# Joining two of three products of the query, key and value projections into one 512-column matmul

## The chip, the cores and the metric

The kernel runs on one core of one Trainium2 chip. The metric is the device time of one execution in microseconds; the time before is a median of three runs. The profile is of one more execution, whose own time stands beside it.

## The reference, cut to what matters

The whole program is one inference step of two trunk layers: a retention and pooling layer and an attention layer, each followed by a feed-forward network (FFN). It works on 9 tiles of 128 tokens: tile 0 holds the context tokens, tiles 1 to 8 the latent tokens. The change lies in the projection of the attention layer, all in float32:

```
def attn_project(h, w_qkv, q_gain, k_gain):
    B, T, _ = h.shape
    q, k, v = jnp.split(h @ w_qkv, [N_HEADS * HEAD_DIM, (N_HEADS + KV_HEADS) * HEAD_DIM], axis=-1)
    q = rmsnorm(q.reshape(B, T, N_HEADS, HEAD_DIM), q_gain)
    k = rmsnorm(k.reshape(B, T, KV_HEADS, HEAD_DIM), k_gain)
    v = v.reshape(B, T, KV_HEADS, HEAD_DIM)
    return q, k, v
```

`h` has 1,152 rows of 1,024 elements, `w_qkv` 1,536 columns: 1,024 for eight query heads, 256 for two key heads and 256 for two value heads. Queries and keys of the latent tokens are then rotated by their place in a grid (`axial_rope`), and the attention follows.

## The kernel before, in words

**Products in parts.** A float32 product is made from parts in the matmul type `fp32r`: each operand is split into a high part (a cast, on ScalarE) and a low part (the rest, a subtraction on VectorE; `split`, lines 155 to 157). `mm3` (line 174) then adds three products into one PSUM region: high by high, high by low, low by high. Its matmuls stand on line 179, which all other stages but the FFN input use too.

**The projection.** The columns of `w_qkv` are taken in six blocks of 256 (`blocks`): value, query heads 0 and 1, key, and three more query blocks. One call of `qkv_step(bi, t)` makes the 256 columns of block `bi` for token tile `t`. The inner dimension of 1,024 is taken in 8 slices of 128, so a step has 8 x 3 = 24 matmuls, each with 128x128 of `h` as the loaded weights and 256 columns of `w_qkv` moving. There are 6 x 9 = 54 steps. The high part of a weight block lies in 2,048 elements of each partition of `RR`, and the low part in the next 2,048; there are two such pairs of regions, and `load_blk` fills one from DRAM through `RAW`, with a cast and a subtraction per half.

**Behind the matmuls.** A step's result stands in one of PSUM's banks of 512 float32 columns (banks 0 to 3 in turn; for the last block 3 and 7) and uses 256 of them. In a value step ScalarE and VectorE split it into `VH` and `VL`; tile 0 is copied to `vctx` and stored. In a query or key step ScalarE squares and sums each head (line 1175), POOL works out the reciprocal root (`rstd_of`, lines 184 and 185), VectorE scales by it and by the gain into `qn` (line 1182), and for latent tokens VectorE and POOL rotate (lines 1190 to 1194) with two temporary halves `ra` and `rb`. Its `tail` (transposes on TensorE, line 1198, and a copy, line 1207) waits in the list `pend` and is issued behind the matmuls of the second step after it. `qn` has three buffers (`qnb`) and `ra`/`rb` two (`rab`), taken in turn.

**Order.** Steps run in two phases. In the first, the value block and the first query block run for three token tiles at a time, while the transposed input `h` is still being made: `go` issues h steps, with transposes on TensorE (line 258), ScalarE's scale and shift into a temporary (line 261) and VectorE's split (lines 263 and 264). In the second phase the other four blocks run over all nine tiles, with the cached keys (line 1223), the cached values and the context's attention between them. In the last block the first score products (`scores`, line 179 again, 512 and 256 columns), with maximum, exponential (line 1291) and so on, run between steps. Within each engine the framework that builds the program arranges the instructions and places all waits; an engine then runs its own queue in order.

Of the kernel before, what the change touches and what calls it, by code (L numbers as in the profile page):

```python
# [17 lines left out]
KD = 8  # L18
# [46 lines left out]
def hybrid_step_kernel(ctx: ExitStack, tc: tile.TileContext, a: dict, outs: list):  # L65
    nc = tc.nc
# [7 lines left out]
    RR = base.tile([128, 26624], F32R, name="RR")  # L74
# [36 lines left out]
    def bank(i, n=1):  # L111
        return PS[:, i * 512:(i + n) * 512]

    def h_hi(g):
        return RR[:, g * 6144:g * 6144 + 3072].rearrange("p (k t) -> p k t", k=KD)

    def h_lo(g):
        return RR[:, g * 6144 + 3072:g * 6144 + 6144].rearrange("p (k t) -> p k t", k=KD)
# [14 lines left out]
    def w_pair(i):  # L133
        b = RR[:, 18432 + i * 2048:18432 + (i + 2) * 2048]
        return (b[:, 0:2048].rearrange("p (k f) -> p k f", k=KD),
                b[:, 2048:4096].rearrange("p (k f) -> p k f", k=KD))

    def tok(t):
        return O[:, :, t * 128:(t + 1) * 128]

# [2 lines left out]
    def sm(n=1):  # L143
        i = ring["sm"]
        if i + n > 64:
            i = 0
        ring["sm"] = i + n
        return SM[:, i:i + n]
# [6 lines left out]
    def split(hi, lo, src):  # L155
        nc.scalar.copy(hi, src)  # L156
        nc.vector.tensor_sub(lo, src, hi)  # L157
# [16 lines left out]
    def mm3(out, items, first=True, last=True):  # L174
        n = 3 * len(items)
        c = 0
        for lh, ll, rh, rl in items:
            for x, y in ((lh, rh), (lh, rl), (ll, rh)):
                nc.tensor.matmul(out=out, lhsT=x, rhs=y, start=(first and c == 0), stop=(last and c == n - 1))  # L179
                c += 1  # L180

    def rstd_of(ss, n, w=1):
        r = sm(w)
        nc.gpsimd.tensor_scalar(r, ss, 1.0 / n, EPS, op0=ALU.mult, op1=ALU.add)  # L184
        nc.gpsimd.tensor_tensor(r, r, nhalf[:, 0:w], op=ALU.pow)  # L185
        return r
# [23 lines left out]
    def chain_steps(t, src, xs, xd, junk, last=False, act=False):  # L210
        if last:
            xb = (XB + [RAW[:, 0], RAW[:, 1]])[t % 4]
        else:
            xb = XB[t] if t < 2 else (XB[0], GB[0], XB[1])[(t - 2) % 3]
        nc.sync.dma_start(out=xb, in_=xs)
        ot = tok(t)
        ss = sm()
        if len(src.shape) == 2:
# [153 lines left out]
    ps = bank(7)  # L372
# [8 lines left out]
    def x_tile(t):  # L381
        x3 = M2[:, 1024 * (t % 4):1024 * (t % 4) + 1024].rearrange("p (k f) -> p k f", k=KD)
        s2 = sm()
        nc.scalar.activation(tok(t), x3, ACTF.Square, accum_out=s2)
        r2 = rstd_of(s2, D)
        nc.vector.tensor_scalar(tok(t), x3, r2, None, op0=ALU.mult)
# [112 lines left out]
    def proj_T(slot, evac, gs=range(NG)):  # L499
        hi, lo = (x.rearrange("p (k f) -> p k f", k=KD) for x in w_unit(slot))  # L500
        for g in gs:
            ps = pb()[:, 0:GT]
            mm3(ps, [(hi[:, k], lo[:, k], h_hi(g)[:, k], h_lo(g)[:, k]) for k in range(KD)])
            evac(g, ps)
            hook()

    def proj_N(wp, evac, before=None):
        hi, lo = wp
        for t in range(NT):
            g, j = divmod(t, 3)  # L510
            if before:
                before(t)
            ps = pb()[:, 0:256]
            js = slice(j * 128, (j + 1) * 128)
            mm3(ps, [(h_hi(g)[:, k, js], h_lo(g)[:, k, js], hi[:, k], lo[:, k]) for k in range(KD)])
            evac(t, ps)
            hook()
# [209 lines left out]
    def out_proj(F, units, order, late, srcs, xs, xd, split_bufs, mid=None):  # L727
# [10 lines left out]
        def mms(t, cs, ks, first, last, n=0):  # L738
            for half in range(2):
                ps = bank(2 * (t % 2) + half)  # L740
                hs = slice(half * 512, half * 512 + 512)
                mm3(ps, [cs[k] + (units[k][0][:, hs], units[k][1][:, hs]) for k in ks], first, last)
                go(n)
# [389 lines left out]
    vctx = XG[:, 2048:2304]  # L1133
    qnb = [XG[:, 2304 + 256 * i:2560 + 256 * i] for i in range(3)]
    rab = [XG[:, 3072 + 512 * i:3584 + 512 * i] for i in range(2)]
# [11 lines left out]
    cnt = {"n": 0, "q": 0}  # L1147
    pend = []

    def qr_buf(bi, t, n):  # L1150
        q, r = qnb[n % 3], rab[n % 2]
        if bi == 5 and t > 3:
            q, r = RAW[:, 0, 256 * (n % 3):256 * (n % 3) + 256], RAW[:, 1, 512 * (n % 2):512 * (n % 2) + 512]
        return q, r[:, 0:256], r[:, 256:512]

    def qkv_step(bi, t):
        kind = blocks[bi][0]
        hi, lo = w_pair(2 * (bi % 2))
        g, j = divmod(t, 3)
        js = slice(j * 128, (j + 1) * 128)  # L1160
        ps = bank(cnt["n"] % 4 if bi < 5 else 3 if t % 2 else 7)[:, 0:256]
        cnt["n"] += 1
        mm3(ps, [(h_hi(g)[:, k, js], h_lo(g)[:, k, js], hi[:, k], lo[:, k]) for k in range(KD)])
        if len(pend) > 1:
            pend.pop(0)()
        if kind == "v":
            if t == 0:
                nc.scalar.copy(vctx, ps)
                nc.gpsimd.dma_start(out=new_cv[0, 0].rearrange("t v d -> t (v d)"), in_=vctx)
            else:  # L1170
                split(VH[:, t - 1], VL[:, t - 1], ps)
            return
        ss = sm(2)
        for e in range(2):
            nc.scalar.activation(jnk[e], ps[:, e * 128:(e + 1) * 128], ACTF.Square, accum_out=ss[:, e:e + 1])
        r = rstd_of(ss, 128, 2)
        cnt["q"] += 1
        n_qn = cnt["q"]
        qn, ra, rb = qr_buf(bi, t, n_qn)
        gain = GQ[:, 128:256] if kind == "k" else GQ[:, 0:128]  # L1180
        for e in range(2):
            nc.vector.scalar_tensor_tensor(qn[:, e * 128:(e + 1) * 128], ps[:, e * 128:(e + 1) * 128], r[:, e:e + 1],
                                           gain, op0=ALU.mult, op1=ALU.mult)
        if t == 0:
            if kind == "k":
                nc.gpsimd.dma_start(out=new_ck[0, 0].rearrange("t v d -> t (v d)"), in_=qn)
        else:
            v3 = lambda x: x.rearrange("p (h d) -> p h d", h=2)
            tb = rope[:, t - 1]
            nc.vector.tensor_mul(v3(ra), v3(qn), tb[:, 0:128].unsqueeze(1).to_broadcast([128, 2, 128]))  # L1190
            nc.gpsimd.tensor_mul(v3(rb), v3(qn), tb[:, 128:256].unsqueeze(1).to_broadcast([128, 2, 128]))
            v4 = lambda x: x.rearrange("p (q x i) -> p q x i", q=4, x=2)
            nc.vector.tensor_add(v4(qn)[:, :, 0], v4(ra)[:, :, 0], v4(rb)[:, :, 1])
            nc.vector.tensor_add(v4(qn)[:, :, 1], v4(ra)[:, :, 1], v4(rb)[:, :, 0])
        def tail(qn=qn, kind=kind, t=t, n=n_qn):
            tp = bank(6 + n % 2 if NT * bi + t < 4 * NT + 6 else 6)[:, 0:256]
            for e in range(2):
                nc.tensor.transpose(tp[:, e * 128:(e + 1) * 128], qn[:, e * 128:(e + 1) * 128], ident)
            tp3 = tp.rearrange("p (h s) -> p h s", h=2)
            if kind == "k":  # L1200
                if t == 0:
                    nc.scalar.copy(kctx, tp)
                else:
                    cs = slice(256 + (t - 1) * 128, 256 + t * 128)
                    split(KR[:, :, 0, cs], KR[:, :, 1, cs], tp3)
            else:
                nc.scalar.copy(O[:, 2 * kind:2 * kind + 2, t * 128:(t + 1) * 128], tp3)

        pend.append(tail)
# [117 lines left out]
    for g in range(NG):  # L1327
        for bi in range(2):
            for t in range(3 * g, 3 * g + 3):
                qkv_step(bi, t)  # L1330
                go(2 if g else 0)
        if g:
            go()
# [5 lines left out]
    for bi in range(2, 6):  # L1339
        for t in range(NT):  # L1340
            qkv_step(bi, t)
            if cf and cf[0][0] <= NT * bi + t:
                cf.pop(0)[1]()
            if bi == 5 and t == 5:
                q_split(0)
            if bi == 5 and t in (6, 7):
                scores(0, t - 6)
            if (bi, t) in side:
                side[bi, t]()
            if (bi, t) in ctx_at:  # L1350
                fa, fb = ctx_pair(ctx_at.index((bi, t)))
                cf += [(NT * bi + t + 2, fa), (NT * bi + t + 3, fb)]
        if bi + 2 < len(blocks):
            load_blk(bi + 2)
# [4 lines left out]
    for n in range(len(pairs)):  # L1359
        if n + 2 < len(pairs):  # L1360
            q_split(n + 2)
        for w in 'T0 v3 S0 T1 v4 T2 S1 T3 V0 V1 T4 V2'.split():
            c, u = w[0], int(w[1])
# [8 lines left out]
        if n % 2 == 1 and 6 <= n // 2 < 14:  # L1372
            k = n // 2 - 6
# [42 lines left out]
```

## Time and profile before

| | us |
|---|---|
| median of 3 runs | 2880.81 (2880.76 to 2882.42) |
| the profiled execution, own time | 2880.93 |
| its span in the profile | 2879.1 |
| busy: TensorE (PE) | 2825.5 |
| busy: VectorE (DVE) | 1789.2 |
| busy: ScalarE (ACT) | 1053.4 |
| busy: GpSimd (POOL) | 299.7 |

The granted TensorE clock was 0.995 of the full one over the execution. In rows of the profile, PEld is TensorE's loading of weights, `128*128` the array part used, `x24` the number of instructions merged in one row, and `[0.62 <-PE PS L179]` at the end of a row is idle time before it and what ended it. A matmul's recorded duration overlaps its neighbours', so that its price is the distance from start to start. All 54 steps lie between about 1495 and 1690 us of the span.

### The profile page before, as it was taken

How to read it: one execution, taken by the hardware profiler on the slowest of the kernel's cores; microseconds unless marked ns; L12 is line 12 of the kernel's file. 1: busy time of each engine (PE TensorE's matmuls, PEld its weight loads, DVE VectorE, ACT ScalarE, POOL GpSimd, SP SyncE). 2: the span in 40 equal slices, each digit the busy share in tenths (PEclk: the TensorE clock that was granted, in tenths of full speed). 3: DMA queues.
4: the chain of work that ended last, by engine and by line, in shares of the span. 5: the costliest groups of instructions: out<-in, count | busy, mean ns of one | idle time of the engine just before them, and what ended most of it. 6: DMA issues, size and time to landing. Idle time of an engine off the chain costs nothing. (4 is left out here: it accounts for less than half of the span.)

```text
span 2879.1 us, 44720 instructions
## 1 busy us (share of the span) xinstructions
PE 2825.5 (98%) x17979; PEld 2547.3 (88%) x17979; DVE 1789.2 (62%) x3008; ACT 1053.4 (37%) x1961; POOL 299.7 (10%) x542
## 2 busy tenths in 40 slices
PE   7999999999999999999999999999999999999998
PEld 5889998788999999977779988888889999998886
DVE  6784455526867676666765567886496555554455
ACT  5232222426322223331253467775362222234111
POOL 2010111111000000000034621110100000000000
PEclk9999999999999999999999999999999999999999
DMA  7531110412333343353341000001233222225222
GB/s 254 170 115 50 36 34 26 142 66 70 114 115 123 107 127 100 126 167 121 121 146 51 23 16 1 23 30 64 87 99 98 73 71 81 75 78 174 78 93 103
DMA packets 194568, 262.59 MB, mean 91 GB/s; under 512 B 10220, under 2 KB 139688, under 8 KB 194232
## 3 DMA queue, kind: packets, MB, share of 16 engines
q1 hardware_dynamic: 182784, 217.88, 24.1%
q0 software_dynamic: 11088, 41.47, 3.8%
q8 instruction: 141, 2.31, 0.3%
q14 instruction: 67, 0.55, 0.1%
q10 hardware_dynamic: 488, 0.38, 0.0%
HBM read 213.52 MB, written 46.17 MB: 90 GB/s over the span
## 5 line engine op out<-in xcount | busy, mean ns | idle before, releaser
L179 PE MATMUL PS<-RR 128*128 128x256 f32 (+2 forms) x6270 | 1130.7, 333 | 1.7 <-ACT RR L156 0.6
L179 PEld LDWEIGHTS PS<-RR 128*128 128x128 f32 x6270 | 956.5, 190 | 117.3 <-issue 19.0
L856 PE MATMUL PS<-RR 128*128 128x288 f32 x5324 | 730.5, 296 | 3.4 <-ACT XGT L871 1.6
L856 PEld LDWEIGHTS PS<-RR 128*128 128x128 f32 x5324 | 714.3, 188 | 12.7 <-ACT O L346 5.9
L156 ACT CAST RR<-O 128x512 fp32r<-128x512 f32 (+1 forms) x242 | 151.8, 627 | 534.4 <-PE PS L856 459.9
L179 PE MATMUL PS<-RR,MID2True 128*128 128x256 f32 (+1 forms) x1416 | 268.9, 338 | 0.1
L1070 DVE TENSOR_TENSOR O<-PS,O 128x512 f32<-128x512 f32 x216 | 148.8, 689 | 172.8 <-PE PS L179 170.6
L179 PEld LDWEIGHTS PS<-RR,MID2True 128*128 128x128 f32 x1416 | 218.2, 189 | 29.9 <-ACT MID1False L724 0.5
L157 DVE TENSOR_TENSOR RR<-O,RR 128x512 fp32r<-128x512 f32 (+1 forms) x242 | 167.5, 693 | 73.4 <-ACT RR L156 73.3
L157 DVE TENSOR_TENSOR RR<-RAW,RR 128x512 fp32r<-128x512 f32 (+1 forms) x119 | 110.3, 931 | 102.5 <-ACT RR L156 79.3
L348 DVE SCALAR_TENSOR_TENSOR O<-O,PW 128x512 f32<-128x512 f32 x224 | 159.6, 744 | 18.0 <-ACT O L346 9.4
L179 PE MATMUL PS<-MID1True,RR 128*128 128x512 f32 (+1 forms) x630 | 166.6, 372 | 2.2 <-ACT XGT L1291 1.7
L156 ACT CAST RR<-RAW 128x512 fp32r<-128x512 f32 (+1 forms) x119 | 95.4, 807 | 196.5 <-PE PS L856 85.3
L856 PE MATMUL PS<-MID1True,RR 128*128 128x288 f32 x1100 | 159.9, 295 | 0.0
L856 PEld LDWEIGHTS PS<-MID1True,RR 128*128 128x128 f32 x1100 | 150.9, 189 | 0.0
L856 PE MATMUL PS<-MID2True,RR 128*128 128x288 f32 x968 | 147.0, 295 | 0.0
L184 POOL TENSOR_SCALAR SM<-SM 128x1 f32<-128x1 f32 (+1 forms) x153 | 57.3, 375 | 782.1 <-ACT PS L220 302.7
L856 PEld LDWEIGHTS PS<-MID2True,RR 128*128 128x128 f32 x968 | 135.5, 189 | 0.0
L887 POOL DMA_DIRECT2D gg<-XGT x44 | 23.6, 536 | 952.8 <-DVE XGT L886 952.8
L1289 DVE TENSOR_REDUCE SM<-PS 128x1 f32<-128x1280 f32 x64 | 95.4, 1491 | 40.5 <-PE PS L179 40.1
L179 PEld LDWEIGHTS PS<-MID1True,RR 128*128 128x128 f32 x630 | 102.6, 189 | 17.6 <-ACT XGT L1291 2.6
L156 ACT CAST RR<-PS 128x512 fp32r<-128x512 f32 x160 | 93.6, 586 | 64.7 <-PE PS L1307 63.5
(295 smaller groups left out, 3090.6 us busy)
## 6 DMA issues: line engine op xcount, KB each, us to landing
O<-in_w_ada_dram SPq DMA_DIRECT2D x68, 512.0 KB
RAW<-in_w_ffn_in_dram SPq DMA_DIRECT2D x100, 256.0 KB
gg<-XGT POOLq DMA_DIRECT2D x44, 576.0 KB, 3.1
O<-in_w_ffn_in_dram SPq DMA_DIRECT2D x92, 256.0 KB
RAW<-in_w_ffn_out_dram SPq DMA_DIRECT2D x30, 512.0 KB
MID2False<-gg SPq DMA_DIRECT2D x26, 576.0 KB
RAW<-in_w_in_even_dram SPq DMA_DIRECT2D x28, 512.0 KB
x<-XGT POOLq DMA_DIRECT2D x27, 512.0 KB, 3.0
```

Of the source, the lines that this page charges most:

```text
L156: nc.scalar.copy(hi, src)
L157: nc.vector.tensor_sub(lo, src, hi)
L179: nc.tensor.matmul(out=out, lhsT=x, rhs=y, start=(first and c == 0), stop=(last and c == n - 1))
L184: nc.gpsimd.tensor_scalar(r, ss, 1.0 / n, EPS, op0=ALU.mult, op1=ALU.add)
L348: nc.vector.scalar_tensor_tensor(self.acc[kind], b[:, k], sv, self.acc[kind], op0=ALU.mult, op1=ALU.add)
L856: nc.tensor.matmul(out=ps, lhsT=u[:, ks], rhs=v, start=first and n == 0, stop=n == 11, skip_group_check=not first)
L887: nc.gpsimd.dma_start(out=gg_scr[self.l][f], in_=XGT[:, 2880:4032])
L1070: nc.vector.tensor_add(dst, p3, dst)
L1289: nc.vector.reduce_max(nm, sp, axis=AX.X, negate=True)
```

## The change

For each slice the products high by high and high by low, which load the same `h` part, become one matmul of 512 columns: its moving operand is the pair of runs high and low (`w_wide`), its output the whole bank. The third, low by high, adds 256 columns to the first half of the bank. Each step has 16 matmuls in place of 24, in the order wide, narrow for the first slice and narrow, wide for the others. Behind them, ahead of the older step's tail, ScalarE copies the second half of the bank to a buffer `x` and VectorE adds the first half to it; all that follows reads `x`. For queries and keys `x` is the buffer that then becomes `qn`; for values it is `vctx` (tile 0) or the first half of one of the `rab` buffers.

```
+    def w_wide(i):
+        return RR[:, 18432 + i * 2048:18432 + (i + 2) * 2048].rearrange("p (x k f) -> p k x f", x=2, k=KD)
...
+    def mm_wide(out, items):
+
+        n = len(items)
+        for i, (lh, ll, rw, rh) in enumerate(items):
+            two_ = [(lh, rw, out.rearrange("p (x f) -> p x f", x=2)), (ll, rh, out[:, 0:256])]
+            for c, (x, y, o) in enumerate(two_ if i == 0 else two_[::-1]):
+                nc.tensor.matmul(out=o, lhsT=x, rhs=y, start=(i == 0 and c == 0), stop=(i == n - 1 and c == 1))
...
-        ps = bank(cnt["n"] % 4 if bi < 5 else 3 if t % 2 else 7)[:, 0:256]
+        ps = bank(cnt["n"] % 4 if bi < 5 else 3 if t % 2 else 7)
         cnt["n"] += 1
-        mm3(ps, [(h_hi(g)[:, k, js], h_lo(g)[:, k, js], hi[:, k], lo[:, k]) for k in range(KD)])
+        ww = w_wide(2 * (bi % 2))
+        mm_wide(ps, [(h_hi(g)[:, k, js], h_lo(g)[:, k, js], ww[:, k], hi[:, k]) for k in range(KD)])
+        if kind == "v":
+            x = vctx if t == 0 else rab[t % 2][:, 0:256]
+        else:
+            cnt["q"] += 1
+            n_qn = cnt["q"]
+            x, ra, rb = qr_buf(bi, t, n_qn)
+        nc.scalar.copy(x, ps[:, 256:512])
+        nc.vector.tensor_add(x, ps[:, 0:256], x)
+        ps = x
         if len(pend) > 1:
             pend.pop(0)()
         if kind == "v":
             if t == 0:
-                nc.scalar.copy(vctx, ps)
                 nc.gpsimd.dma_start(out=new_cv[0, 0].rearrange("t v d -> t (v d)"), in_=vctx)
...
         r = rstd_of(ss, 128, 2)
-        cnt["q"] += 1
-        n_qn = cnt["q"]
-        qn, ra, rb = qr_buf(bi, t, n_qn)
+        qn = x
```

## The prediction

> **What bounds the kernel now.** I read the page's header and engine totals first, then the windows table over the projection stage, then what TensorE waits for there, then the timeline of single steps.
>
> ```profile
> span 2879.1 us, 44720 instructions
> PE 2825.5 (98%) x17979; PEld 2547.3 (88%) x17979; DVE 1789.2 (62%) x3008; ACT 1053.4 (37%) x1961; POOL 299.7 (10%) x542
> ```
>
> TensorE is busy for 98% of the span; no other engine is near it. So what TensorE no longer has to do comes off the span, unless it waits instead. The changed step runs 54 times (6 blocks of 256 columns, 9 token tiles), between about 1495 and 1690 us. The windows table (us; busy time and count per engine):
>
> ```profile
> core 0: us, PE busy (x) PEld busy (x) DVE busy (x) ACT busy (x) POOL busy (x), PEclk, DMA share, GB/s
> 1495.00:1521.00 26.00, 22.82 (x189) 22.24 (x188) 16.53 (x36) 13.24 (x32) 13.47 (x16) 1.00 0.39 132
> 1521.00:1541.00 20.00, 20.00 (x172) 20.00 (x171) 12.43 (x32) 8.96 (x26) 4.95 (x9) 1.00 0.01 1
> 1541.00:1669.00 128.00, 126.84 (x1054) 125.53 (x1053) 74.08 (x209) 49.33 (x219) 73.40 (x111) 1.00 0.10 31
> 1669.00:1690.00 21.00, 17.78 (x116) 14.76 (x116) 12.52 (x28) 10.89 (x28) 7.45 (x14) 1.00 0.14 51
> ```
>
> From 1521 to 1669 TensorE is full but for 1.2 us, at the whole clock (PEclk 1.00). VectorE is at 58% there and ScalarE at 39%: both have room on average. The two ends have waits, listed here by waiter and releaser (total, times, longest):
>
> ```profile
> PE PS L258 <- ACT XGT L261: 3.2, 2, 1.7
> PE PS L179 <- ACT XGT L1291: 1.7, 2, 0.9
> PE PS L1223 <- DVE MID1True L157: 0.8, 1, 0.8
> PE PS L1198 <- DVE RAW L1194: 0.7, 1, 0.7
> PE PS L179 <- DVE RAW L1182: 0.5, 1, 0.5
> ...
> PE PS L1198 <- DVE XGT L1194: 0.3, 1, 0.3
> ```
>
> One ordinary step, timeline (start, duration, engine, line, operation):
>
> ```profile
> 1611.08 0.38 PE L1198 MATMUL PS<-CT,XGT 128*128 128x128 f32 x2
> 1611.22 3.12 PE L179 MATMUL PS<-RR 128*128 128x256 f32 x24
> 1611.42 0.28 ACT L1175 ACTIVATE XGT<-PS 128x128 f32<-128x128 f32 x1 [2.25 <-DVE XGT L1190]
> 1611.68 0.36 ACT L1207 COPY O<-PS 128x256 f32<-128x256 f32 x1
> ...
> 1612.40 0.19 POOL L184 TENSOR_SCALAR SM<-SM 128x2 f32<-128x2 f32 x1 [0.48 <-ACT XGT L1175]
> 1612.67 0.69 POOL L185 TENSOR_TENSOR SM<-SM,PW 128x2 f32<-128x2 f32 x1
> ...
> 1613.40 0.61 DVE L1182 SCALAR_TENSOR_TENSOR XGT<-PS,SM,XGT 128x128 f32<-128x128 f32 x2 [0.96 <-POOL SM L185]
> ...
> 1614.18 0.38 PE L1198 MATMUL PS<-CT,XGT 128*128 128x128 f32 x2
> ...
> 1615.32 0.28 DVE L1194 TENSOR_TENSOR XGT<-XGT 128x128 f32<-128x128 f32 x1
> ...
> 1617.26 0.38 PE L1198 MATMUL PS<-CT,XGT 128*128 128x128 f32 x2
> ```
>
> The step whose matmuls end at 1611.08 passes through ScalarE (squares), POOL (root), VectorE (scaling, rotation) and is ready at 1615.60. Its transposes run after the matmuls of two more steps, at 1617.26. So this chain takes 4.52 us of 6.18: 1.66 us of slack.
>
> **The change part by part.**
>
> *Matmuls removed and widened.* Per inner slice three 256-column matmuls become one of 512 and one of 256. Narrow price: a run of 96 lies between two pairs of transposes, 11.59 us from its start to the next pair; the run of 24 above takes 2.96 us (1611.22 to 1614.18). The 72 more take 8.63 us, 119.9 ns each, and 0.08 us is left over in both, for the first matmul after transposes.
>
> ```profile
> 1541.70 11.76 PE L179 MATMUL PS<-RR 128*128 128x256 f32 x96
> 1553.29 0.38 PE L1198 MATMUL PS<-CT,XGT 128*128 128x128 f32 x2
> ```
>
> Wide price: the last layer's FFN output is a run of 512-column matmuls, one piece in the chain of waits; and the first score products are six of 512 and three of 256 in mixed order:
>
> ```profile
> 2593.34 228.09 PE PS L179 x996
> ...
> 1668.84 2.00 PE L179 MATMUL PS<-MID1True,RR 128*128 128x512 f32 x9
> 1670.68 3.04 PE L179 MATMUL PS<-RR 128*128 128x256 f32 x24
> ```
>
> The first gives 228.09/996 = 229.0 ns; the second 1.84 us, less 0.08 for the start and 3 x 0.12, over six: 233 ns. I take 231 ns. A slice then costs 231 + 119.9 = 350.9 ns against 359.7: 8.8 ns less. There are 54 x 8 = 432 slices: 432 x 8.8 = 3.8 us. With 229 ns it is 4.7 us, with 233 ns 2.9 us. The moving operand of the wide matmul is two runs of 256 that lie 2,048 elements apart; the rows read here don't show whether that has a price. Were the two runs worth no more than two narrow matmuls (239.8 ns), the gain is nothing. I see no reason for more than that, nor for less than 229.
>
> What joining saves is thus only the small fixed part of one matmul (239.8 against 231).
>
> *Added: a ScalarE copy and a VectorE addition per step*, 54 of each, 128x256 out of PSUM. The copy has its row above (0.36 us, L1207). The addition's nearest row is a 128x256 VectorE subtraction that also reads PSUM and SBUF, below: 0.42 us. Neither engine is the bound: 54 x 0.36 = 19.4 us more on ScalarE and 22.7 us on VectorE spread over 190 us, where the windows leave both about half free. What counts is that they are two more links ahead of the squares, 0.8 us with the handovers, in a chain with 1.66 us to spare. In the ordinary step this is covered; without that cover it would be 45 query and key steps x 0.8 us = 36 us. It isn't covered where the chain is late already: at the three tail or cache transposes of the waits above (0.8, 0.7 and 0.3 us). At 0.8 us each that is 2.4 us at most, and nothing if what they wait for last is another chain; no row decides it, so I take the middle, 1.2 us, and 0 to 2.4 for the range. Queued behind a late copy on ScalarE are the next tail's copy and, while weights are loaded, a cast.
>
> *Moved: the PSUM bank comes free after the addition*, not after the scaling (L1182): some 1.5 us sooner. What hangs on it now is one wait, L179 on L1182, 0.5 us, where the score products need the bank of the last block. I take it as gone, -0.5 us; what is late next there are the last tail's transposes, counted above.
>
> *Buffers.* Query and key steps evacuate into the buffer that held the scaled result anyway, three of them, last read by transposes a step earlier: no wait. Value steps take half of a rotation buffer, and the last query step before the fourth (and the seventh) value step still reads that half. Rows around the fourth value step (whose evacuation starts at 1521.24) and the h transposes that share the time:
>
> ```profile
> 1521.24 0.37 ACT L156 CAST MID2True<-PS 128x256 fp32r<-128x256 f32 x1 [2.13 <-PE PS L179]
> ...
> 1522.18 0.28 DVE L1194 TENSOR_TENSOR XGT<-XGT 128x128 f32<-128x128 f32 x1
> 1522.39 0.42 DVE L157 TENSOR_TENSOR MID2True<-PS,MID2True 128x256 fp32r<-128x256 f32 x1
> ...
> 1523.78 0.67 ACT L261 ACTIVATE XGT<-PS,modT,SC 128x384 f32<-128x384 f32 x1 [1.32 <-DVE RR L264]
> 1524.48 0.36 DVE L263 CAST RR<-XGT 128x384 fp32r<-128x384 f32 x1 [0.82 <-ACT XGT L261]
> ...
> 1524.79 0.82 PE L258 MATMUL PS<-CT,O 128*128 128x128 f32 x6
> 1524.88 0.56 DVE L264 TENSOR_TENSOR RR<-XGT,RR 128x384 fp32r<-128x384 f32 x1
> ...
> 1525.56 0.67 ACT L261 ACTIVATE XGT<-PS,modT,SC 128x384 f32<-128x384 f32 x1 [0.19 <-DVE RR L264]
> ```
>
> The copy of that value step must wait until 1522.46 (end of L1194) instead of 1521.24: 1.2 us, with ScalarE's tail copy and the h evacuation (L261) behind it, and TensorE's next h transposes behind that. The h steps go one at a time through ScalarE 0.67, VectorE 0.36 and 0.56: 1.78 us from one L261 to the next, 3.56 us for the two that TensorE takes between value steps, just what TensorE takes itself. So this stretch has no slack, each addition can push it by 0.42 us, and what TensorE saves in these five steps (5 x 0.07 us) is lost. Bounds: 0 to 1.2 + 4 x 0.42 = 2.9 us. VectorE is free while L261 runs, which is 0.67 us, room enough for one addition; so I take 0.5 us, and 0.4 us for the lost saving here and in the first steps (TensorE waits 3.2 us for L261 there as it is). The first value tile's store, issued from POOL, follows the addition, not the copy; behind it on POOL stands the root of the last token tile, whose h transposes run 15 us later: I cost it at nothing.
>
> *A port rule that speaks against the change.* The scaling now has two SBUF inputs, not PSUM and SBUF. In the step above it starts at 1613.40 when POOL has just ended (1613.36), and POOL's next work waits for it: nothing overlaps, so nothing is added.
> The Trainium skill (SBUF — State Buffer, "Who interferes with whom") says that a VectorE instruction with two SBUF inputs and a GpSimd instruction that reads SBUF block each other. By it the value subtraction and the scaling could hold POOL up for their own length. No run so far shows this for the changed pair.
>
> *Sum:* -3.8 + 1.2 - 0.5 + 0.5 + 0.4 = -2.2 us. The profiled execution took 2880.93 us, 0.12 us over the median 2880.81 of the runs, so 2878.7 by the one and 2878.6 us by the other. All in favour: -4.7 - 0.5 = -5.2, 2875.6 us. All against: 0 + 2.4 + 2.9 + 0.4 = +5.7, 2886.5 us.
>
> **The rivals.** A measurement of this kernel can tell about 0.2%, 5.8 us, from no change.
>
> 1. *The wide matmul is worth two narrow ones* (239.8 ns), as far as the two runs of its operand or its order with narrow ones cost what joining saves. Then only the added links remain: +1.2 - 0.5 + 0.5 = +1.2 us, 2882.0 us. For it: 233 in mixed order against 229 in a pure run. Against: both are below 239.8. Chance 0.15.
> 2. *Weight loads are the bound*, and a third of them goes: each matmul that disappears gives back its whole 119.9 ns, 432 x 119.9 = 51.8 us, 2829 us. For it: weight loading is busy for 88% of the span. Against: 512 columns cost 229 to 233 ns with one load each; were loads the bound, they would cost about what 256 do. Chance 0.03.
> The Trainium skill (TensorE: Matmul & The Clock Gate, "Back-to-back issue gap") gives a sustained 131 ns for 512 columns. With the row's 119.9 ns for the narrow one, a slice would be an estimated 251 ns, 47 us less in all. The trace disagrees: 229 ns over 996 of them.
> 3. *Slower: the chain outgrows its slack.* The two links are queued in order on ScalarE and VectorE behind split work. If they lengthen the chain by over 1.66 us and what the steps shorten, each of 45 steps makes TensorE wait at its transposes for what is over. At 2.0 us instead of 0.8 that is 45 x 0.34, with 0.14 more for two shorter steps, 21 us: 2898 us; the sign turns at 1.6 us. For it: two handovers between busy queues. Against: both are half free. Chance 0.08.
> 4. *A better fit:* the order on each engine is arranged by the framework and not the source's (the tail copy above runs between the two squares), so it is arranged anew; should the joins at both ends also lose the 1.7 us (score products for L1291) and the 1.8 us of late transposes: -3.8 - 0.5 - 3.5 = -7.8 us, 2873.0 us. For it: banks come free sooner. Against: those waits are for chains that grow. Chance 0.14.
>
> **How the numbers follow.** The forecast has 0.60. Its own range is 2875.6 to 2881, with the tails of its costs to 2884. Rival 1 lies inside; the range reaches down towards rival 4 and up over most of the costs against: 2874 to 2885 us. Left out are rivals 2 and 3 and the lower half of 4, below 0.2. Faster by over 0.2%: rival 2, nearly all of rival 4: 0.16. Slower: rival 3 and the top of the costs: 0.10. Within: 0.74.
>
> **What would show it.** Right: 432 matmuls of 512 columns on a new line, 231 ns start to start, and 432 of 256; a step from one transpose pair to the next shorter by 0.07 us; the L1182 wait gone; the tail transposes' waits up by under 1 us each; h transposes late by some tenths near 1522 us. Wrong: a wide matmul under 220 or over 240 ns, transposes waiting in ordinary steps, or a span moved by stages outside 1495 to 1690 us.

## The result, and the profile after

The changed kernel is slower: 2923.26 us median (2921.9 to 2925.68, 4 runs) against 2880.78 us (2880.08 to 2882.42, 4 runs) of the kernel before beside it; the ratio is 1.0145, with a 95% interval of 1.0133 to 1.0157. The forecast was 2878.6 us, in a range of 2874 to 2885 us. Some 42 us were lost where 2 us were expected to be won.

The page's header and engine totals, then the windows table over the projection stage, after:

```profile
span 2923.9 us, 43927 instructions
PE 2837.0 (97%) x17547; PEld 2530.9 (87%) x17547; DVE 1808.3 (62%) x3062; ACT 1073.6 (37%) x2014; POOL 295.3 (10%) x542
```

```profile
core 0: us, PE busy (x) PEld busy (x) DVE busy (x) ACT busy (x) POOL busy (x), PEclk, DMA share, GB/s
1498.00:1546.00 48.00, 42.38 (x246) 36.37 (x246) 30.98 (x73) 25.06 (x64) 16.46 (x22) 0.96 0.21 72
1546.00:1720.00 174.00, 140.99 (x782) 116.91 (x782) 93.71 (x265) 68.55 (x278) 71.40 (x117) 0.97 0.08 23
1720.00:1740.00 20.00, 18.15 (x104) 15.36 (x104) 14.74 (x26) 10.58 (x21) 5.73 (x10) 0.88 0.15 53
```

TensorE has 432 instructions fewer, as the change says, and yet in the middle stretch it stands idle for 33 of 174 us, where before it was full. VectorE (54%) and ScalarE (39%) are no fuller than before: no engine has become the bound by its work. The transposes of the steps' tails date the stage. The view by line gives min/median/max ns and first and last start, before and then after:

```profile
L1198 PE MATMUL PS<-CT,XGT x80: 270/272/331, 1518.0 to 1665.3; 128*128 128x128 f32 x80
L1198 PE MATMUL PS<-CT,RAW x10: 272/273/328, 1668.7 to 1685.1; 128*128 128x128 f32 x10
```

```profile
L1216 PE MATMUL PS<-CT,XGT x80: 270/273/332, 1520.1 to 1703.5; 128*128 128x128 f32 x80
L1216 PE MATMUL PS<-CT,RAW x10: 272/273/328, 1707.6 to 1730.7; 128*128 128x128 f32 x10
```

From the first to the last tail it is 167.1 us before and 210.6 us after: 43.5 of the 44.8 us by which the span grew lie here. What TensorE waits for there, after (us in all, times, longest):

```profile
PE PS L1216 <- DVE XGT L1212: 25.1, 22, 2.2
PE PS L269 <- ACT XGT L272: 5.6, 4, 1.5
PE PS L182 <- ACT XGT L1309: 4.7, 2, 4.3
PE PS L1216 <- ACT XGT L1195: 2.9, 1, 2.9
```

The tail transposes (L1216) wait for the rotation's last addition (L1212), in 22 of the 45 query and key steps. So the chain that the prediction gave 1.66 us of slack is late in ordinary steps, by up to 2.2 us. The timeline of one step shows why. L1183 is the join's addition, L1195 the squares, L195 and L196 the root, L1200 the scaling, L1208 to L1212 the rotation:

```profile
1559.67 0.42 DVE L1183 TENSOR_TENSOR XGT<-PS,XGT 128x256 f32<-128x256 f32 x1
1560.13 0.31 ACT L1195 ACTIVATE XGT<-XGT 128x128 f32<-128x128 f32 x1 [1.12 <-DVE XGT L1183]
...
1560.44 0.38 PE L1216 MATMUL PS<-CT,XGT 128*128 128x128 f32 x2
...
1560.73 0.35 ACT L1182 COPY XGT<-PS 128x256 f32<-128x256 f32 x1
...
1561.19 0.70 POOL L196 TENSOR_TENSOR SM<-SM,PW 128x2 f32<-128x2 f32 x1
1561.92 0.62 DVE L1200 SCALAR_TENSOR_TENSOR XGT<-XGT,SM 128x128 f32<-128x128 f32 x2 [1.82 <-POOL SM L196]
1562.57 0.43 DVE L1208 TENSOR_TENSOR XGT<-XGT 128x256 f32<-128x256 f32 x1
1562.61 0.98 POOL L1209 TENSOR_TENSOR XGT<-XGT 128x256 f32<-128x256 f32 x1 [0.73 <-DVE XGT L1200]
...
1563.83 0.28 DVE L1212 TENSOR_TENSOR XGT<-XGT 128x128 f32<-128x128 f32 x1
1564.03 0.42 DVE L1183 TENSOR_TENSOR XGT<-PS,XGT 128x256 f32<-128x256 f32 x1
```

The next step's matmuls ended at 1560.44 and ScalarE's copy of their second half was done at 1561.08. Its addition could have run then, while VectorE stood idle for 1.82 us waiting for POOL. It ran at 1564.03, since in VectorE's queue it stands behind the scaling and rotation of the step before. And its own squares, root, scaling and rotation all wait for it. So one step's chain cannot begin before the last step's has ended: the chain has become a loop, with a period of 1564.03 - 1559.67 = 4.36 us, and TensorE's steps of 3.1 us wait for it. Before the change the squares read PSUM and did not wait for the last step's rotation: in the step of the prediction's timeline they start at 1611.42, and the rotation of the step before ends only at 1612.44, so that two chains overlapped.

```profile
1612.16 0.28 DVE L1194 TENSOR_TENSOR XGT<-XGT 128x128 f32<-128x128 f32 x1
```

The loop isn't in every step. In the last four blocks 28 of the 35 distances from one addition (L1183) to the next are 4.34 us or more. The other seven are 2.8 to 3.9 us: there the framework put the addition ahead of the last step's rotation, or the last step was that of token tile 0, which has none.

Theory A is this loop through VectorE's queue. Theory B: two more links make the chain too long for its slot, whatever engine they are on. Theory C: the wide matmul is at fault.

### The profile page after: what moved, and what is told of

It reads as the page before. It is cut to its first block, busy times and chain, and to the rows that moved or that the text cites. A ratio compares the mean times of both kernels' runs of the same rounds, so it can differ in the third digit from the quotient of the medians.

```text
span 2923.9 us, 43927 instructions
## 1 busy us (share of the span) xinstructions
PE 2837.0 (97%) x17547; PEld 2530.9 (87%) x17547; DVE 1808.3 (62%) x3062; ACT 1073.6 (37%) x2014; POOL 295.3 (10%) x542
## 5 line engine op out<-in xcount | busy, mean ns | idle before, releaser
L182 PE MATMUL PS<-RR 128*128 128x512 f32 (+2 forms) x4974 | 964.6, 345 | 1.8 <-ACT O L1079 0.7
L182 PEld LDWEIGHTS PS<-RR 128*128 128x128 f32 x4974 | 798.8, 190 | 117.0 <-issue 19.0
L867 PEld LDWEIGHTS PS<-RR 128*128 128x128 f32 x5324 | 715.5, 189 | 12.6 <-ACT O L357 5.9
L191 PE MATMUL PS<-RR 128*128 128x256 f32 (+1 forms) x864 | 169.3, 350 | 0.0
L191 PEld LDWEIGHTS PS<-RR 128*128 128x128 f32 x864 | 136.8, 195 | 18.4 <-DVE XGT L1183 0.2
L195 POOL TENSOR_SCALAR SM<-SM 128x1 f32<-128x1 f32 (+1 forms) x153 | 53.6, 351 | 824.2 <-ACT PS L231 302.7
L1307 DVE TENSOR_REDUCE SM<-PS 128x1 f32<-128x1280 f32 x64 | 95.5, 1492 | 43.0 <-PE PS L182 42.5
```

The source lines that it names most:

```text
L191: nc.tensor.matmul(out=o, lhsT=x, rhs=y, start=(i == 0 and c == 0), stop=(i == n - 1 and c == 1))
L867: nc.tensor.matmul(out=ps, lhsT=u[:, ks], rhs=v, start=first and n == 0, stop=n == 11, skip_group_check=not first)
L1307: nc.vector.reduce_max(nm, sp, axis=AX.X, negate=True)
```

## The experiments

**The join without the wide matmul.** The high by low product goes to the second half of the bank in narrow matmuls, and the join stays:

```
-            two_ = [(lh, rw, out.rearrange("p (x f) -> p x f", x=2)), (ll, rh, out[:, 0:256])]
+            three = [(lh, rh, out[:, 0:256]), (lh, rw[:, 1], out[:, 256:512]), (ll, rh, out[:, 0:256])]
```

> The join alone: 24 narrow matmuls a step, as before, with the high by low product sent to the second half of the bank, then the copy and the addition of the changed kernel. Theory A (queue loop: VectorE's addition of a step stands in its queue behind the rotation of the step before, and the squares wait for it, so that a step lasts the whole chain from addition to addition, 4.35 us, not TensorE's 3.1): the wide matmul has no part in the loss, about 2920 to 2928 us. Theory C (the wide matmul is at fault): about 2881 to 2884 us.

Measured: 2924.52 us, ratio to before 1.0149 (1.0132 to 1.0166). The whole loss is there without a wide matmul: theory C falls.

**The wide matmul without the join.**

```
-        nc.scalar.copy(x, ps[:, 256:512])
-        nc.vector.tensor_add(x, ps[:, 0:256], x)
-        ps = x
+        ps = ps[:, 0:256]
```

> The wide matmul alone: 16 matmuls a step, and all that follows reads the first half of the bank, as before. It leaves out the high by low product, which is made and never added. Theories A and B: the saving on TensorE alone, 3 to 5 us, 2876 to 2878 us. Theory C: about 2923 us.

Measured: 2879.78 us, ratio 0.9995 (0.9986 to 1.0004): the loss is gone, and the expected 3 to 5 us less can't be told from none by these runs (the interval reaches from -4.0 to +1.2 us).

**One link on ScalarE, one link on VectorE.** In the kernel before, query and key results are first copied to the scaling's buffer, in one kernel by ScalarE, in the other by VectorE:

```
+        if kind != "v":
+            cnt["q"] += 1
+            n_qn = cnt["q"]
+            qn, ra, rb = qr_buf(bi, t, n_qn)
+            nc.scalar.copy(qn, ps)        # the other kernel: nc.vector.tensor_copy(qn, ps)
+            ps = qn
```

> The kernel before with one more link in the chain of query and key steps: ScalarE copies the 256 result columns to the scaling's buffer, and squares and scaling read that copy. Theory A: no loop through VectorE's queue, so 0 to 5 us over before, 2881 to 2886 us. Theory B (any link counts, as the chain outgrows its slack of 1.66 us): 0.4 us more is inside the slack, so about the same here, and the same as for the link on VectorE.

> The same single link, but the copy is VectorE's (0.4 us). Theory A: the squares now wait for an instruction that stands behind the last step's rotation, so nearly the whole loss, 2915 to 2925 us. Theory B: as the link on ScalarE, at most 2886 us.

Measured: 2881.28 us with ScalarE's copy, ratio 1.0002 (0.9992 to 1.0011), and 2924.09 us with VectorE's, 1.0149 (1.0134 to 1.0164). Links of the same length (0.37 and 0.42 us) at the same place in the chain: one costs nothing that can be measured, the other all of it. Theory B falls; what counts is whose queue the link stands in. First the timeline of the kernel with VectorE's copy (L1168; squares L1181, scaling L1185, the rotation's last addition L1197):

```profile
1574.70 0.28 DVE L1197 TENSOR_TENSOR XGT<-XGT 128x128 f32<-128x128 f32 x1
1574.91 0.42 DVE L1168 COPY XGT<-PS 128x256 f32<-128x256 f32 x1
...
1575.42 0.31 ACT L1181 ACTIVATE XGT<-XGT 128x128 f32<-128x128 f32 x1 [2.51 <-DVE XGT L1168]
...
1577.20 0.62 DVE L1185 SCALAR_TENSOR_TENSOR XGT<-XGT,SM 128x128 f32<-128x128 f32 x2 [1.88 <-POOL SM L185]
...
1579.11 0.28 DVE L1197 TENSOR_TENSOR XGT<-XGT 128x128 f32<-128x128 f32 x1
1579.31 0.41 DVE L1168 COPY XGT<-PS 128x256 f32<-128x256 f32 x1
```

It is the same loop, 4.40 us from copy to copy. The kernel with ScalarE's copy (L1168 again):

```profile
1573.54 0.38 PE L1201 MATMUL PS<-CT,XGT 128*128 128x128 f32 x2
...
1573.78 0.37 ACT L1168 COPY XGT<-PS 128x256 f32<-128x256 f32 x1 [1.90 <-POOL SM L185]
...
1574.31 0.32 ACT L1181 ACTIVATE XGT<-XGT 128x128 f32<-128x128 f32 x1
...
1574.93 0.28 DVE L1197 TENSOR_TENSOR XGT<-XGT 128x128 f32<-128x128 f32 x1
...
1576.63 0.38 PE L1201 MATMUL PS<-CT,XGT 128*128 128x128 f32 x2
```

Here the squares (1574.31) start before the last step's rotation ends (1575.21): the chains overlap, and a step takes 3.09 us.

**Scaling and rotation issued behind the next step's addition.** The changed kernel, with this part of the step put in a function that the next step calls after its join:

```
+        def rest():
...
+        late.append(rest)
```

> The changed kernel with one thing moved: scaling and rotation of a query or key step are issued one step later, behind the next step's addition (wide matmuls, copy and addition as they are; the transposes stay two steps back). Theory A: the addition no longer stands behind the rotation of the step before, the loop is cut and nearly all of the 42 us come back; left over are some tenths of waiting per step, since scaling now starts about 0.9 us later and the transposes come when they did: 2878 to 2895 us. Theory B (the chain is too long for its slot): the chain is longer still, no gain, 2920 us or more.

> As the run before, and the transposes of a step come one step later as well (three steps back; the context's last piece moves by one step with them). Theory A: the loop is cut and the chain has one step more: TensorE's saving of 3 to 4 us shows, 2876 to 2882 us. Theory B: this lengthens the slot by 3.1 us, so it gains what theory A says, but then the run before must not.

Measured: 2921.84 us, ratio 1.0141 (1.0126 to 1.0156), and with the later transposes 2922.19 us, 1.0144 (1.0129 to 1.0159). No gain, as theory B would have it. But the trace shows that the order did not change. The second of the two (addition L1185, squares L1199, scaling L1205, the rotation's last addition L1217):

```profile
1615.92 0.28 DVE L1217 TENSOR_TENSOR XGT<-XGT 128x128 f32<-128x128 f32 x1
...
1616.42 0.42 DVE L1185 TENSOR_TENSOR XGT<-PS,XGT 128x256 f32<-128x256 f32 x1 [0.22 <-ACT XGT L1184]
1616.88 0.31 ACT L1199 ACTIVATE XGT<-XGT 128x128 f32<-128x128 f32 x1 [0.49 <-DVE XGT L1185]
...
1618.67 0.61 DVE L1205 SCALAR_TENSOR_TENSOR XGT<-XGT,SM 128x128 f32<-128x128 f32 x2 [1.82 <-POOL SM L196]
```

The addition still stands behind the rotation, and the scaling that follows is its own step's: the framework had arranged the queue as it was. (The 0.22 us are a wait for ScalarE's copy of the same step; the next additions, at 1620.78, 1625.13 and 1629.48, follow at the loop's distance.) Even three steps of slot did not help, since a loop's period has nothing to do with how late its result may be. These two runs didn't test what they were to test.

**Control: the same move in the kernel before.**

> Control: the kernel before with the same move of scaling and rotation, no join and no wide matmul. Theory A: there was no loop to cut, so no gain: 2880 to 2890 us, the upper end if the later scaling makes transposes wait.

Measured: 2883.27 us, ratio 1.0007 (0.9997 to 1.0016): no loss that can be measured. (In it the scaling of the last block's token tile 7 reads its bank after score products have overwritten it.) Its trace shows that here, too, the order is the old one: a scaling (L1187) at 1604.72 comes right behind the root of its own step, which ends at 1604.68, and ahead of the next step's squares at 1605.82. So it tells little.

**The value block alone** with wide matmuls and join:

```
+        if kind == "v":
+            mm_wide(ps, [(h_hi(g)[:, k, js], h_lo(g)[:, k, js], ww[:, k], hi[:, k]) for k in range(KD)])
...
+            mm3(ps, [(h_hi(g)[:, k, js], h_lo(g)[:, k, js], hi[:, k], lo[:, k]) for k in range(KD)])
```

> Wide matmul and join in the value block's nine steps alone; queries and keys as before. Theory A: in a value step nothing waits for anything behind the addition but its own split, so no loss: 2879 to 2883 us. If the value steps' buffers (shared with the rotation) carry part of the loss, as the prediction priced them, up to 2884 us.

Measured: 2882.80 us, ratio 1.0005 (0.9996 to 1.0015). The value steps, and the buffers that they share with the rotation, have at most some 4 us of the loss (the interval reaches from -1.2 to +4.3 us). What they do shows in the waits of the h transposes, which were 3.2 us before:

```profile
PE PS L269 <- ACT XGT L272: 4.5, 3, 1.5
```

**The order held.** The two kernels in which scaling and rotation were moved, now with both tied behind the addition on VectorE, and a third like the second but with narrow matmuls:

```
+        join = nc.vector.tensor_add(x, ps[:, 0:256], x)
...
+            with tc.issue_after(join):
+                late.pop(0)()
```

> The move of the run join_first had been undone by the framework's own arrangement: in its trace the addition still stood behind the rotation of the step before. Now each step's scaling and rotation are tied behind the next step's addition on VectorE, so that the order holds. Transposes two steps back. Theory A: the loop is cut: 2878 to 2895 us, with some tenths of waiting per step at the transposes. If it stays at 2920 us, theory A falls: then the order in VectorE's queue isn't what makes the step long.

> The same tie, and the transposes three steps back. Theory A: TensorE's saving shows, 2876 to 2882 us; below the kernel before if nothing else waits.

> As the run before, but with 24 narrow matmuls a step (the high by low product into the second half of the bank). Against that run this shows the price of the matmuls alone: 3 to 4 us more than it.

Measured: 2891.62 us with the transposes two steps back, ratio 1.0034 (1.0022 to 1.0047); 2879.49 us with three, 0.9992 (0.9983 to 1.0001); and 2882.61 us with three and narrow matmuls, 1.0004 (0.9995 to 1.0013). The two wide ones differ from the changed kernel in order alone, and 32 and 44 us come back. (Against the kernel before, the faster of them can't be told from no change: the interval reaches from -4.9 to +0.3 us.) The second one's timeline (addition L1185, scaling L1208, squares L1202, last addition L1220):

```profile
1601.58 0.38 PE L1227 MATMUL PS<-CT,XGT 128*128 128x128 f32 x2
...
1602.68 0.42 DVE L1185 TENSOR_TENSOR XGT<-PS,XGT 128x256 f32<-128x256 f32 x1 [0.53 <-ACT XGT L1184]
1603.02 0.60 DVE L1208 SCALAR_TENSOR_TENSOR XGT<-XGT,SM 128x128 f32<-128x128 f32 x2
1603.14 0.31 ACT L1202 ACTIVATE XGT<-XGT 128x128 f32<-128x128 f32 x1 [0.49 <-DVE XGT L1185]
...
1604.62 0.38 PE L1227 MATMUL PS<-CT,XGT 128*128 128x128 f32 x2
...
1604.92 0.28 DVE L1220 TENSOR_TENSOR XGT<-XGT 128x128 f32<-128x128 f32 x1
...
1605.71 0.42 DVE L1185 TENSOR_TENSOR XGT<-PS,XGT 128x256 f32<-128x256 f32 x1 [0.51 <-ACT XGT L1184]
```

The addition now waits for ScalarE's copy of its own step alone. While VectorE scales the step before (1603.02), ScalarE squares the new one (1603.14): the chains overlap again. A step takes 3.04 us (1601.58 to 1604.62), against 3.10 us before. With the transposes two steps back, the later scaling leaves them waiting:

```profile
PE PS L1227 <- DVE XGT L1220: 9.5, 14, 1.0
```

That is the part of the story that theory B had right: once the loop is cut, the length of the chain against its slot is what remains, about 10 us. Wide against narrow, all else alike, is 2879.49 against 2882.61 us: 3.1 us less.

## Why the prediction was wrong, point by point

**The step that failed** is "*Added: a ScalarE copy and a VectorE addition per step*", where it says "two more links ahead of the squares, 0.8 us with the handovers, in a chain with 1.66 us to spare. In the ordinary step this is covered". The chain of one step was held against its slot, as though only its length counted. But one of the links is an instruction of VectorE, whose queue at that point is taken by the step before until 1.4 us after the matmuls end: the row was quoted (L1194 at 1615.32, ending at 1615.60, with the matmuls' end at 1614.18) and read only as the end of a chain. By rows that were there, the new chain could have been closed to a loop: addition 0.42, squares to the root's end 1.94 (1611.42 to 1613.36), scaling to the last addition 2.20 us (1613.40 to 1615.60), 4.56 us without handovers, against a step of 3.1. The tails of the last four blocks show what the loop cost there. Their 36 pairs of transposes lay 3.40 us apart on average before (1565.90 to 1684.95; 3.09 in an ordinary step, more where caches, context and score products come between) and 4.38 us after (1577.27 to 1730.55), close to the loop's 4.36. That is 34.2 of the 43.5 us between the first and the last tail; the other 9.2 us lie in the first phase, where the tails wait for the rotation too and the h transposes and the lower clock (last section) add to it.

**Queued behind.** The same paragraph named what is queued behind the copy on ScalarE. It did not ask what VectorE's addition is queued behind, nor who waits for it; the two runs with a single link show that this question alone decides between 0 and 43 us.

**The matmuls' price was right.** 350.9 ns for a wide and a narrow one against 359.7 for three narrow ones gave 3.8 us. In the changed kernel a run of 64 matmuls, four steps, lies between two pairs of transposes:

```profile
1549.16 11.44 PE L191 MATMUL PS<-RR 128*128 128x512 f32 x64
```

The next pair starts at 1560.44, so the run takes 11.28 us; less the 0.08 us of its start this is 350.0 ns a slice. The two tied kernels that differ in nothing but the matmuls show 3.1 us (11 runs of each, 2877.6 to 2881.22 against 2880.23 to 2883.95 us). The wide matmul without the join showed 1.2 us, in an interval that holds both 3.8 us and nothing.

**The PSUM bank and the score products' wait.** The wait of 0.5 us for the scaling went, as forecast, but in its place the score products waited 4.7 us instead of 1.7 us for the exponential (L1309). It is the tail of the loop: the row maximum ahead of the exponential (L1307, at 1714.59) stands in VectorE's queue behind a scaling that waits for its root until 1714.06, and TensorE stands still from about 1713.3 to 1717.63.

**The buffers** shared between value steps and rotation were priced at 0.5 us, 0 to 2.9. With the value block alone the h transposes wait 1.3 us more (4.5 against 3.2): inside those bounds, and too little for the whole time to show.

**The scaling's two SBUF inputs** were costed at nothing, and nothing was added: the scaling of a head took 350 ns (median) against 348 before, POOL's product 966 against 976 ns.

**Rivals.** The third had the right sign. It took the chain's length for the cause and put 2898 us and a chance of 0.08 on it; the cause was a loop, which needs no delay behind split work. That its 2898 us lies nearer to the measured time than the forecast is luck: it added up what a chain exceeds its slot by, and the loss is a loop's period in place of a step. The second (weight loads as the bound) is refuted: 432 loads fewer gave some 3 us. The first (nothing gained by widening) isn't borne out by the 3.1 us. The fourth's waits grew instead of going.

## What to carry to other kernels

Before an instruction is put at the head of a chain that repeats step by step, look at what its engine's queue holds at that moment: if work of the step before stands there and ends the same chain, the steps can no longer overlap, and their period is the whole chain, however idle the engine is. VectorE was 54% busy here. The same link on an engine whose queue held no end of the chain cost nothing that could be measured (2881.28 us against 2880.96). And where a framework arranges the queues, a move in the source proves nothing until the trace shows the new order: here the tie was worth 30 us with the transposes two steps back and 43 us with three, the move alone 1.4 us at most.

## What the hardware showed that was not expected

TensorE's clock was not whole in the changed stage: from the first to the last tail the granted clock was 0.97 of the full one, before the change 1.00. TensorE is idle there for 33 us more than before (37.2 against 4.0) and busy for 10 us more (173.5 against 163.1), though it has fewer matmuls. In the windows table (columns as above), the changed kernel:

```profile
1530.00:1533.50 3.50, 3.41 (x13) 3.03 (x14) 2.45 (x6) 1.61 (x5) 0.00 (x0) 0.55 0.02 5
```

Here the granted clock is 0.55, and a step's 16 matmuls (L191) take longer than in the step before. TensorE's timeline at this place and at a second one:

```profile
1523.90 3.04 PE L191 MATMUL PS<-RR 128*128 128x512 f32 x16
1528.05 0.55 PE L269 MATMUL PS<-CT,O 128*128 128x128 f32 x3 [1.11 <-ACT XGT L272]
1530.09 0.70 PE L269 MATMUL PS<-CT,O 128*128 128x128 f32 x3 [1.49 <-ACT XGT L272]
1530.44 4.58 PE L191 MATMUL PS<-RR 128*128 128x512 f32 x16
```

```profile
1606.74 0.44 PE L1216 MATMUL PS<-CT,XGT 128*128 128x128 f32 x2 [2.04 <-DVE XGT L1212]
1606.94 3.03 PE L191 MATMUL PS<-RR 128*128 128x512 f32 x16
1611.84 0.44 PE L1216 MATMUL PS<-CT,XGT 128*128 128x128 f32 x2 [1.87 <-DVE XGT L1212]
1612.03 4.59 PE L191 MATMUL PS<-RR 128*128 128x512 f32 x16
```

A step of 3.04 us becomes one of 4.6, after waits of which none was longer than 2.04 us: in both places two of them stand close together, with six transposes between and behind them or with one step's matmuls between. A third slow step (4.47 us, at 1684.48) follows a single wait of 2.85 us. But this isn't a rule: waits of 2.16 and 1.40 us (at 1569.57 and 1574.20), also with one step's matmuls between, and a single one of 2.07 us (at 1644.52) were each followed by steps of some 3.1 us. The three slow steps together are 4.5 us longer. How much the clock adds to the loss wasn't tested: where TensorE waits for the loop anyway, a slower step is partly hidden. In the tied kernel with the later transposes the clock is 1.00 from 1510 to 1680 us, and the loss is gone. The Trainium skill (TensorE: Matmul & The Clock Gate, "HAM oscillation — how this bites in real kernels") warns of idle gaps of more than some 3.4 us; the two places here had shorter ones. A wait of 4.35 us agrees with it: the score products behind it start at 1717.63, and the granted clock is 0.57 from 1717.6 to 1721.0. The Trainium skill, on the same page ("A second HAM failure mode: psum-queue depth-cycling"), tells of short idles between groups of matmuls that come often enough to lower the clock, and that is nearer to these rows.
